# A two-layer RWKV-7 and attention block on one core: the readout products of a chain step ordered behind those of its state

## The chip, the cores and the metric

The kernel runs on 1 core of a Trainium2 chip. The metric is the device time in microseconds (us) of one execution; the median of three runs stands for it. One more execution was taken with the hardware profiler, and every row shown comes from that one.

A core has five engines that run side by side, each with a queue of its own that it works off in order: PE multiplies matrices (PEld are its weight loads), DVE works on vectors, ACT applies functions and copies, POOL is a second, general engine, and SP here only issues DMA transfers. PE writes to PSUM, a small memory that DVE and ACT read; everything else lies in SBUF or, outside the core, in DRAM.

## The reference, cut to what matters

The block has two layers on one residual stream of 1024 latent tokens and 256 context tokens, 1024 channels wide. Layer 0 mixes the tokens with a bidirectional RWKV-7 recurrence, layer 1 with attention; each is followed by an MLP. The change touches the recurrence of layer 0 alone, which the reference writes as a scan over tokens, for 16 heads of 64 channels, forward and backward:

```python
def _wkv_step(state, inp):
    r, w, k, v, kk, bvec = inp
    sa = jnp.einsum('bhvk,bhk->bhv', state, -kk)
    state = state * w[:, :, None, :] + sa[..., None] * bvec[:, :, None, :] + v[..., None] * k[:, :, None, :]
    y = jnp.einsum('bhvk,bhk->bhv', state, r)
    return state, y

def _rwkv_scans(p, init_f, init_b):
    r, v, g, kk, dirs = p
    (dec_f, k_f, a_f), (dec_b, k_b, a_b) = dirs
    s_f, y_f = wkv_scan(r, dec_f, k_f, v, kk, kk * a_f, init_f, False)
    s_b, y_b = wkv_scan(r, dec_b, k_b, v, kk, kk * a_b, init_b, True)
    return s_f, s_b, y_f + y_b
```

## The kernel before

The scan over single tokens is replaced by one over chunks of 32 tokens: 40 chunks (8 of the context, 32 latent), each a *step* of a *chain*. The 16 heads are cut into four groups of four (two channel tiles `ct2` by two halves `h`), and a `Chain` (line 820) carries one group forward and backward at once. So a step works on eight units: two tiles, two halves, two directions `d`. Two chains run side by side, first groups 0 and 1, then groups 2 and 3: 160 steps in all.

A step (`Chain.step`, line 838) has four products of PE, each of eight calls, one for each unit. In fp32 the trace shows two instructions for one call.

- **X** (line 854): the chunk's inputs against the stacked rows `SV`, which hold the state (64 rows), the values V and the corrections U. It goes to `ps_x`, and ACT copies it to SBUF (line 856).
- **U** (line 860): X times an inverse 32 by 32 triangular matrix `T`. It goes to the other half of `ps_x`. Four copies, one for each 32 partitions, put it into `SV` (line 867, ACT, in the first half of a pass one of the four on DVE).
- **S** (line 874): the next state, from all rows of `SV`, into `ps_s`. DVE multiplies it with the decay and writes it into the state rows of the next `SV` (line 878, one instruction for each half). It isn't needed in the last step.
- **Y** (line 883): the readout of the step, from the same `SV`, into `ps_y`. ACT copies it to `y` (line 886), or, once the other direction has been there, DVE adds it (line 888).

X, U and Y are calls with 32 columns of weights, S with 64; all contract over 128 rows. The next step's X needs the new state; nothing in the chain needs Y.

`T` is the inverse spread over a matrix that is zero outside its 32 partitions (`inverses`, line 831, POOL). It is made for step s + 1 once step s has used its own, since each of the two chains has one buffer of it (`bp`, line 785).

The buffers in PSUM: `px` with two for X and U, `pss` with two for S, `py` with one for Y (line 786), beside three that others hold at that time: eight banks in all.

The data of two steps is loaded at once (`Lanes.load`, line 805): `ST` (1152 KB: the inputs of both chains, with the inverses), `LS` (twice 256 KB: weights of S) and `SV` (eight times 32 KB: the rows V), 11 DMA issues on SP. Each has two buffers, so the load for the next pair can go out when the last step that read the same buffer is done with it: `LS` when S is, `SV` and `ST` when Y is.

What sets the order: `staggered` (line 912) starts the second chain half a step behind the first, and `weave` (line 209) mixes in other work: while groups 0 and 1 run, the rest of the preparation (`Prep`: products, vector work and inverses for the later groups); while groups 2 and 3 run, parts of the readout (`Readout`: centring and scaling of y). The order of each engine's queue isn't this program order, though: a scheduler picks it when the kernel is built, from a simulated timeline, by program order among what is ready then. `k.order(late, early)` (line 136) ties one instruction behind another in that choice, without a semaphore.

Of the kernel before, what the change touches and what calls it, by code (L numbers as in the profile page):

```python
# [9 lines left out]
F32 = mybir.dt.float32  # L10
# [101 lines left out]
class K:  # L112


    def __init__(self, tc, I, O, ctx, dbg):
        self.tc, self.nc, self.I, self.O, self.ctx, self.dbg = tc, tc.nc, I, O, ctx, dbg
        self.const = ctx.enter_context(tc.tile_pool(name="const", reuse_waits="tile", bufs=1))
        self.dram = ctx.enter_context(tc.tile_pool(name="dram", reuse_waits="tile", bufs=1, space=DRAM))
        self.c, self.S, self.tables = {}, {}, None
        self.trail = collections.deque(maxlen=LAG)  # L120
# [654 lines left out]
class Lanes:  # L775
# [3 lines left out]
    def __init__(self, k, es):  # L779
        tc, nc = k.tc, k.nc  # L780
        sb = lambda n, b: es.enter_context(tc.tile_pool(name=n, reuse_waits="tile", bufs=b))
        ps = lambda n, b: es.enter_context(tc.tile_pool(name=n, reuse_waits="tile", bufs=b, space=PSUM))
        vp = sb("vp", 1)
        self.gp, self.xp = sb("gp", 2), sb("xp2", 2)
        self.bp = sb("bp", 1)
        self.px, self.pss, self.py = ps("px", 2), ps("pss", 2), ps("py", 1)
        self.SV = [vp.tile([128, 2, 2, 4, 2, 64], F32, name=f"SV{b}", tag=f"SV{b}") for b in range(2)]
        self.LS = [vp.tile([128, 2, 2, 2, 2, 64, 2], F32, name=f"LS{b}", tag=f"LS{b}") for b in range(2)]
        for b, a, h in itertools.product(range(2), range(2), range(2)):
            q = QUAD[a, h] * 32  # L790
            nc.vector.memset(self.SV[b][q:q + 32, h, a], 0.0)
        for t in self.LS:
            for h in range(2):
                rows = slice(h * 64, h * 64 + 64)
                eye = k.c["ident"][rows, rows].unsqueeze(1).unsqueeze(3).to_broadcast([64, 8, 64, 2])
                nc.scalar.copy(t[rows, h].rearrange("p l d a e c -> p (l d a) e c"), eye)
        self.ST = {}
# [22 lines left out]
class Chain:  # L820
# [17 lines left out]
    def step(self, s):  # L838
        k, nc, pr, L = self.k, self.k.nc, self.pr, self.L
        i, c = divmod(s, 2)  # L840
        both = lambda c: slice(c, 4 - c, 3 - 2 * c)
        gf, gb = self.seq[i]
        rev, lp, ln = gf > gb, pr // 2, pr % 2
        ST, ls, SV = L.ST[lp, i], L.LS[i % 2], L.SV[i % 2]
        stack = lambda ct2, h, d, o: ST[:, ln, h * 4 + ct2 * 2 + d, c, o:o + 32]
        sv = lambda h, ct2, d: SV[:, h, ct2, 2 * d + (c ^ d), ln, :]
        units = [(ct2, h, d) for d in range(2) for ct2 in range(2) for h in range(2)]
        if s == 0:
            self.inverses(0)
        T = self.T  # L850
        xu = L.px.tile([128, 2, 2, 64], F32, name="ps_x", tag="xu")
        for ct2, h, d in units:
            q = QUAD[ct2, h] * 32
            nc.tensor.matmul(xu[q:q + 32, 0, d, :], stack(ct2, h, d, 0), sv(h, ct2, d), start=True, stop=True, tile_position=(0, q))  # L854
        X = L.xp.tile([128, 2, 64], F32, name="X", tag=f"X{ln}")
        L.copied = nc.scalar.copy(X, xu[:, 0])
        yield
        for ct2, h, d in units:
            q = QUAD[ct2, h] * 32
            nc.tensor.matmul(xu[q:q + 32, 1, d, :], T[:, d, q // 32, :], X[:, d, :], start=True, stop=True, tile_position=(0, q))  # L860
        lo, hi = sorted((2 * gf + c, 2 * gb + 1 - c))
        first = lo not in self.seen
        self.seen |= {lo, hi}
        for ct2 in range(2):
            for h in range(2):
                q = QUAD[ct2, h] * 32
                (nc.vector.tensor_copy if first and ct2 == h == 0 else nc.scalar.copy)(SV[q:q + 32, h, ct2, both(c), ln, :], xu[q:q + 32, 1])  # L867
        yield
        if s + 1 < self.n:
            self.inverses(s + 1)  # L870
            i2, c2 = divmod(s + 1, 2)
            pst = L.pss.tile([128, 2, 2, 64], F32, name="ps_s", tag="s")
            for ct2, h, d in units:
                nc.tensor.matmul(pst[h * 64:h * 64 + 64, ct2, d, :], ls[:, h, ln, d, ct2, :, c], sv(h, ct2, d), start=True, stop=True, tile_position=(0, h * 64))  # L874
            for h in range(2):
                rows = slice(h * 64, h * 64 + 64)
                pt = k.c["PT"][rows, pr * 2:pr * 2 + 2, :, s + 1].unsqueeze(3).to_broadcast([64, 2, 2, 64])
                nc.vector.tensor_tensor(L.SV[i2 % 2][rows, h, :, both(c2), ln, :], pst[rows], pt, ALU.mult)  # L878
        yield
        psy = L.py.tile([128, 2, 64], F32, name="ps_y", tag="y")  # L880
        for ct2, h, d in units:
            q = QUAD[ct2, h] * 32
            L.last = nc.tensor.matmul(psy[q:q + 32, d ^ rev, :], stack(ct2, h, d, 32), sv(h, ct2, d), start=True, stop=True, tile_position=(0, q))  # L883
        o = self.y[:, lo:hi + 1:hi - lo, :]
        if first:
            nc.scalar.copy(o, psy)
        else:
            nc.vector.tensor_tensor(o, o, psy, ALU.add)
# [606 lines left out]
```

## Time and profile before

| | |
|---|---|
| median of 3 runs | 4176.76 us (4176.29 to 4187.85) |
| profiled execution | 4175.26 us, its span 4173.5 us |
| PE busy | 3815.4 us (91%) |
| DVE busy | 2206.2 us (53%) |
| ACT, POOL busy | 1503.9 us, 1493.4 us (36% each) |
| DMA, mean over the span | 99 GB/s |
| mean granted clock of PE | 0.922 |

The span is the time from the first to the last instruction of the profiled execution; busy times are of that span. The granted clock is the share of its full speed at which PE was allowed to run. A row of the timeline has the start in us, the length in us, the engine, the line of the kernel, the operation, what is written and read, the shapes and the count of instructions that were merged; in brackets stands how long the engine had been idle before and what ended that. A row of the waits has who waited for whom, the us in total, how many times and the longest. The chain steps run from 862 to 1570 us of the span; ahead of them lie projections and preparation, behind them the output projection, the MLP and the second layer.

### The profile page before, as it was taken

The page shows a single profiled execution, that of the slowest core. Times are in us where ns is not written, and L with a number is a line of the kernel's source. Part 1 is how long each engine was busy: PE and PEld are TensorE (multiplying, and loading weights), DVE is VectorE, ACT ScalarE, POOL GpSimd, SP SyncE. Part 2 cuts the span into 40 slices and gives each one's busy share as a digit, 9 for nine tenths or more (in the row PEclk, how much of TensorE's full clock was granted, in tenths as well). Part 3 has the DMA queues.
Part 4 walks back from the last instruction along what each step waited for, and adds up shares of the span by engine and source line. Part 5 has one row for each costly group of instructions (what it writes and reads, how often), then busy time and mean ns, then how long its engine had stood idle before and what let it go on. Part 6 is the DMA issues. An engine that isn't in the chain of part 4 may idle for free.

```text
span 4173.5 us, 70565 instructions
## 1 busy us (share of the span) xinstructions
PE 3815.4 (91%) x28100; PEld 2915.1 (70%) x28100; DVE 2206.2 (53%) x3705; ACT 1503.9 (36%) x3215; POOL 1493.4 (36%) x1395
## 2 busy tenths in 40 slices
PE   6999768767898998999999999989999999999998
PEld 3667647655666666888888888776444477888886
DVE  6347898878745446443333333648666534333324
ACT  4666555444243333322222222333444422221122
POOL 3124785644424233311111111123778722222221
PEclk8999868856598989999999999999999999999999
DMA  7457867776454444401111111433110021111112
GB/s 276 150 182 178 201 154 173 176 186 155 119 173 134 135 126 133 146 27 39 39 40 39 38 38 39 162 84 108 31 31 16 19 78 41 48 44 48 48 51 71
DMA packets 398202, 414.78 MB, mean 99 GB/s; under 512 B 153504, under 2 KB 303264, under 8 KB 392624
## 3 DMA queue, kind: packets, MB, share of 16 engines
q1 hardware_dynamic: 396912, 408.94, 34.2%
q8 instruction: 222, 3.64, 0.4%
q0 software_dynamic: 960, 1.31, 0.2%
q14 instruction: 108, 0.88, 0.1%
HBM read 294.99 MB, written 117.11 MB: 99 GB/s over the span
## 4 chain that ended last, share of the span: by engine, by line
PE 62%; DVE 5%; DMA 2%; ACT 1%; issue 1%; POOL 0%; SPq 0%; DVEq 0%; POOLq 0%; ACTq 0%
PE ps_pj L271 43%; PE ps_av L1361 4%; PE ps_s L874 3%; PE ps_m L1238 2%; PE ps_s L1401 2%; PE ps_pj L290 2%; PE ps_s L1402 2%; PE ps_y L883 2%; DVE SV L878 2%; PE ps_x L854 1%; DMA ro_v<-d_V 0%; PE ps_su L1372 0%; PE ps_q L1275 0%; POOL w_lo L255 0%; DMA SV<-d_V 0%
## 5 line engine op out<-in xcount | busy, mean ns | idle before, releaser
L255 POOL TENSOR_TENSOR w_lo<-w_raw,w_hi 128x512 fp32r<-128x512 f32 (+1 forms) x292 | 478.3, 1639 | 1693.1 <-ACT w_hi L253 1671.8
L271 PE MATMUL ps_pj<-xh,w_hi 128*128 128x512 f32 (+1 forms) x1712 | 626.7, 367 | 6.4 <-ACT w_hi L253 6.0
L271 PE MATMUL ps_pj<-xl,w_hi 128*128 128x512 f32 (+1 forms) x1712 | 622.5, 364 | 1.0 <-DVE xl L1004 1.0
L271 PE MATMUL ps_pj<-xh,w_lo 128*128 128x512 f32 (+1 forms) x1712 | 617.6, 364 | 5.3 <-POOL w_lo L255 5.2
L1119 DVE SCALAR_TENSOR_TENSOR xr<-ps_pj,c_mod,xr 128x512 f32<-128x512 f32 (+1 forms) x368 | 251.9, 686 | 577.1 <-PE ps_pj L271 576.4
L253 ACT CAST w_hi<-w_raw 128x512 fp32r<-128x512 f32 (+1 forms) x292 | 216.7, 742 | 843.8 <-PE ps_pj L271 626.5
L271 PE MATMUL ps_pj<-hid_l,w_hi 128*128 128x512 f32 (+1 forms) x1280 | 474.4, 371 | 0.0
L271 PE MATMUL ps_pj<-hid_h,w_hi 128*128 128x512 f32 (+1 forms) x1280 | 473.2, 371 | 0.0
L271 PE MATMUL ps_pj<-hid_h,w_lo 128*128 128x512 f32 (+1 forms) x1280 | 469.8, 370 | 0.0
L1143 DVE TENSOR_TENSOR m_q<-m_r 128x512 f32<-128x512 f32 x160 | 183.8, 1150 | 418.2 <-ACT m_r L1141 417.9
L271 PEld LDWEIGHTS ps_pj<-xh,w_hi 128*128 128x128 f32 x1712 | 324.5, 190 | 61.1 <-ACT w_hi L253 7.8
L271 PEld LDWEIGHTS ps_pj<-xh,w_lo 128*128 128x128 f32 x1712 | 322.4, 189 | 59.1 <-POOL w_lo L255 8.1
L271 PEld LDWEIGHTS ps_pj<-xl,w_hi 128*128 128x128 f32 x1712 | 324.3, 190 | 53.4 <-DVE xl L1004 1.8
L1412 POOL TENSOR_TENSOR acc<-acc,p 128x1024 f32<-128x1024 f32 x122 | 295.4, 2421 | 58.8 <-ACT p L1405 54.4
L874 PE MATMUL ps_s<-SV,LS 128*64 128x64 f32 x2496 | 248.1, 266 | 30.9 <-DVE SV L867 23.8
L271 PEld LDWEIGHTS ps_pj<-hid_h,w_hi 128*128 128x128 f32 x1280 | 241.3, 189 | 44.2
L271 PEld LDWEIGHTS ps_pj<-hid_h,w_lo 128*128 128x128 f32 x1280 | 241.1, 188 | 43.9
L271 PEld LDWEIGHTS ps_pj<-hid_l,w_hi 128*128 128x128 f32 x1280 | 241.4, 189 | 43.2
L878 DVE TENSOR_TENSOR SV<-ps_s,c_PT 64x256 f32<-64x256 f32 x312 | 131.4, 421 | 228.4 <-PE ps_s L874 222.4
L1405 ACT ACTIVATE p<-ps_s 128x1024 f32<-128x1024 f32 x160 | 163.8, 1024 | 230.5 <-PE ps_s L1402 229.8
L271 PE MATMUL ps_pj<-xlo,w_hi 128*128 128x512 f32 (+1 forms) x576 | 226.0, 393 | 12.6 <-DVE xlo L480 12.5
L874 PEld LDWEIGHTS ps_s<-SV,LS 128*64 128x64 f32 x2496 | 170.5, 161 | 90.2 <-DVE SV L867 30.0
(235 smaller groups left out, 7269.8 us busy)
## 6 DMA issues: line engine op xcount, KB each, us to landing
ST<-d_ST SPq DMA_DIRECT2D x40, 1152.0 KB
wmod<-in_wmod SPq DMA_DIRECT2D x32, 1024.0 KB
w_raw<-in_m SPq DMA_DIRECT2D x64, 512.0 KB
w_raw<-in_m SPq DMA_DIRECT2D x128, 256.0 KB
d_ST<-AR SPq DMA_DIRECT2D x160, 128.0 KB
d_LS<-KT SPq DMA_DIRECT2D x320, 64.0 KB
d_ST<-G SPq DMA_DIRECT2D x160, 128.0 KB
LS<-d_LS SPq DMA_DIRECT2D x80, 256.0 KB
```

Source lines behind the costliest of these rows:

```text
L253: nc.scalar.copy(hi, raw)
L255: getattr(nc, eng).tensor_tensor(lo, raw, hi.bitcast(F32), ALU.subtract)
L271: i = nc.tensor.matmul(ps[:, :n], w[:, sl], x[:, t0:t0 + n], start=a, stop=z)
L290: nc.tensor.matmul(ps[:, :n], w[:, sl], x[:, t0:t0 + n], start=a, stop=z)
L874: nc.tensor.matmul(pst[h * 64:h * 64 + 64, ct2, d, :], ls[:, h, ln, d, ct2, :, c], sv(h, ct2, d), start=True, stop=True, tile_position=(0, ...
L878: nc.vector.tensor_tensor(L.SV[i2 % 2][rows, h, :, both(c2), ln, :], pst[rows], pt, ALU.mult)
L883: L.last = nc.tensor.matmul(psy[q:q + 32, d ^ rev, :], stack(ct2, h, d, 32), sv(h, ct2, d), start=True, stop=True, tile_position=(0, q))
L1119: k.nc.vector.scalar_tensor_tensor(x[:, t0:t0 + n], ps[:, :n], g, x[:, t0:t0 + n], ALU.mult, ALU.add)
L1143: nc.vector.tensor_tensor(q[:, :n], r[:, :n], r[:, :n], ALU.mult)
L1361: line(nc.tensor.matmul(st["av"][e * 64:e * 64 + 64], k.V[:, kt, ct // 2 * 64:ct // 2 * 64 + 64], p[:, e], start=(kt == 0), stop=(kt == 9) ...
L1405: nc.scalar.activation(p, ps, AF.Exp)
L1412: (nc.vector if ct == KT - 1 and kt % 3 == 2 else nc.gpsimd).tensor_tensor(st["acc"], st["acc"], p, ALU.add)
```

## The change

It does three things.

1. Each Y call of a step is ordered behind the last S call of that step (where there is one).
2. Y gets no tile of its own: it is written into a third part of the tile that holds X and U. The pool `py` goes, and `px` has three buffers in place of two.
3. The pool `bp` of `T` has two buffers in place of one.

```diff
         self.gp, self.xp = sb("gp", 2), sb("xp2", 2)
-        self.bp = sb("bp", 1)
-        self.px, self.pss, self.py = ps("px", 2), ps("pss", 2), ps("py", 1)
+        self.bp = sb("bp", 2)
+        self.px, self.pss = ps("px", 3), ps("pss", 2)
...
-        xu = L.px.tile([128, 2, 2, 64], F32, name="ps_x", tag="xu")
+        xu = L.px.tile([128, 3, 2, 64], F32, name="ps_x", tag="xu")
...
             pst = L.pss.tile([128, 2, 2, 64], F32, name="ps_s", tag="s")
             for ct2, h, d in units:
-                nc.tensor.matmul(pst[h * 64:h * 64 + 64, ct2, d, :], ls[:, h, ln, d, ct2, :, c], sv(h, ct2, d), start=True, stop=True, tile_position=(0, h * 64))
+                last = nc.tensor.matmul(pst[h * 64:h * 64 + 64, ct2, d, :], ls[:, h, ln, d, ct2, :, c], sv(h, ct2, d), start=True, stop=True, tile_position=(0, h * 64))
...
         yield
-        psy = L.py.tile([128, 2, 64], F32, name="ps_y", tag="y")
+        psy = xu[:, 2]
         for ct2, h, d in units:
             q = QUAD[ct2, h] * 32
-            L.last = nc.tensor.matmul(psy[q:q + 32, d ^ rev, :], stack(ct2, h, d, 32), sv(h, ct2, d), start=True, stop=True, tile_position=(0, q))
+            i = nc.tensor.matmul(psy[q:q + 32, d ^ rev, :], stack(ct2, h, d, 32), sv(h, ct2, d), start=True, stop=True, tile_position=(0, q))
+            if s + 1 < self.n:
+                k.order(i, last)
```

## The prediction

> **What bounds the kernel now.** I read the page first: PE ends the run and holds most of the chain that ended last.
>
> ```profile
> span 4173.5 us, 70565 instructions
> PE 62%; DVE 5%; DMA 2%; ACT 1%; issue 1%; POOL 0%; SPq 0%; DVEq 0%; POOLq 0%; ACTq 0%
> ```
>
> The diff touches only the chain steps, which run between 862 and 1570 us, so the rest of the page can't move by itself. I cut that stretch into seven stages (A to G, in this order) and counted X's copy, L856, which stands once in each of the 160 chain steps. Columns: stretch, its length, ACT busy (count), granted clock, DMA share, GB/s.
>
> ```profile
> 862.00:1147.00 285.00, 10.19 (x40) 0.60 0.61 150
> 1147.00:1215.00 68.00, 6.65 (x25) 1.00 0.58 177
> 1215.00:1302.00 87.00, 6.59 (x26) 0.96 0.51 156
> 1302.00:1374.00 72.00, 3.84 (x16) 0.74 0.39 117
> 1374.00:1505.00 131.00, 9.83 (x39) 1.00 0.45 139
> 1505.00:1552.00 47.00, 2.57 (x10) 0.64 0.46 137
> 1552.00:1570.00 18.00, 1.27 (x5) 1.00 0.28 83
> ```
>
> Length over count is the price of a step: A 7.1 us, B 2.7, C 3.35, D 4.5, E 3.36, F 4.7, G 3.6. C, E and G repeat one pattern. This is one step of it, from X to the next X, in the timeline of E (each call of fp32 stands as two instructions, so x16 is one set of eight calls):
>
> ```profile
> 1405.85 0.44 PE L860 MATMUL ps_x<-X,T 128*32 128x64 f32 x13
> 1406.23 0.30 PE L854 MATMUL ps_x<-SV,ST 128*32 128x64 f32 x2
> 1406.66 0.30 DVE L867 COPY SV<-ps_x 32x128 f32<-32x128 f32 x1
> 1406.99 0.82 ACT L867 COPY SV<-ps_x 32x128 f32<-32x128 f32 x3 [0.63 <-DVE SV L867]
> 1407.04 0.33 PE L874 MATMUL ps_s<-SV,LS 128*64 128x64 f32 x2
> 1407.31 0.30 PE L883 MATMUL ps_y<-SV,ST 128*32 128x64 f32 x2
> 1407.72 0.25 ACT L856 COPY X<-ps_x 128x128 f32<-128x128 f32 x1
> ...
> 1408.52 0.57 PE L874 MATMUL ps_s<-SV,LS 128*64 128x64 f32 x10
> 1409.02 0.45 SPq L813 DMA_DIRECT2D LS<-d_LS  x1
> 1409.03 0.35 PE L883 MATMUL ps_y<-SV,ST 128*32 128x64 f32 x9
> 1409.13 0.88 DVE L878 TENSOR_TENSOR SV<-ps_s,c_PT 64x256 f32<-64x256 f32 x2 [2.17 <-PE ps_s L874]
> 1409.60 0.30 PE L854 MATMUL ps_x<-SV,ST 128*32 128x64 f32 x2
> ```
>
> See that S (L874, 64 columns) and Y (L883, 32 columns) take turns, one call each: three turns in 1.48 us (1407.04 to 1408.52), 0.49 each; only then do five calls of S stand together. S takes 1407.04 to 1409.03, 1.99 us. It isn't the U copies that pace the turns: they end some 0.27 us apart (0.82 for three) and are all done at 1407.81. And DVE waits 2.17 us for S before it can form the next state. Stage B shows the same instructions without turns, in the chain that comes second:
>
> ```profile
> 1191.44 0.70 PE L874 MATMUL ps_s<-SV,LS 128*64 128x64 f32 x16
> 1192.08 0.49 PE L854 MATMUL ps_x<-SV,ST 128*32 128x64 f32 x16
> 1192.46 0.43 PE L883 MATMUL ps_y<-SV,ST 128*32 128x64 f32 x16
> 1192.79 0.30 PE L854 MATMUL ps_x<-SV,ST 128*32 128x64 f32 x2
> ```
>
> There a whole S takes 0.64 us up to the next form, a whole Y 0.33.
>
> **The change part by part.**
>
> **Y behind S.** No instruction is added. Eight Y calls move behind the last S call of their step, so the three turns go. The wait is one of order on PE alone; behind Y stands U of the other chain, which needs X's copy and that isn't late (1407.72). Y also releases the SV and ST buffers to SP: it now ends some 0.5 us behind S, while SP is at the two issues of LS (1.09 us, below): covered. S and Y cost 0.64 + 0.33 = 0.97 us of PE, against 1.99 plus the five Y calls that already stand behind (5/8 of 0.33, 0.21): 2.20. That is 1.2 us less PE a step at full clock. Not all of it is time, for two loops come next.
>
> The first is the loop through the copies: U's end, four copies in a row (1406.66 to 1407.81, 1.15 us), the five S calls that need the last copy (0.51 with the change of form), Y 0.33, the next U 0.44, and some 0.1 for hand-overs: 2.5 us. In half of the steps the first copy sits on DVE behind L878; with 0.2 more there I take 2.6.
>
> The second is the load of the next pair of steps, which has two buffers: LS goes out when the last S that reads the buffer is done, and then ST and SV.
>
> ```profile
> 1181.77 0.43 PE L854 MATMUL ps_x<-SV,ST 128*32 128x64 f32 x9 [0.33 <-DMA SV<-d_V]
> 1192.17 1.09 SPq L813 DMA_DIRECT2D LS<-d_LS  x2
> 1201.30 1.42 POOL L836 TENSOR_TENSOR T<-ST,c_qmask 128x256 f32<-128x256 f32 x2 [5.78 <-DMA ST<-d_ST]
> 1202.94 0.49 PE L854 MATMUL ps_x<-SV,ST 128*32 128x64 f32 x16
> ```
>
> From LS's issue ST has landed after 9.1 us (1192.17 to 1201.30), SV comes behind it, and X starts after 10.8; at 1181.77 it already waits 0.33 for SV. So the load takes between 9.2 and 10.7 us. In E the next LS starts 2.8 us behind an X (1406.23 to 1409.02) and four steps of 3.37 make 13.5: 10.7 are left, so the load is only just hidden. After the change S ends about 1.1 us behind X (X 0.38, S 0.64, a hand-over), and four steps can't be under 1.1 + 9.2 to 1.1 + 10.7, 10.3 to 11.8: 2.6 to 2.95 a step. I take 2.85, nearest to the row in which X waits. C and E: 65 steps by 0.5, **32.5 us** (between 65 by 0.3 and by 0.85). G has no load behind it: 5 by 0.7, **3.5**. In B one chain of two takes turns and the load is the limit already (10.9 for four): 0.1 by 25, **2.5** (0 to 9).
>
> Stages A, D and F have other work on DVE and a clock that falls to half. What a step pays there:
>
> ```profile
> 1351.69 1.12 PE L874 MATMUL ps_s<-SV,LS 128*64 128x64 f32 x16
> ...
> 1527.81 0.48 PE L874 MATMUL ps_s<-SV,LS 128*64 128x64 f32 x2
> 1530.92 0.53 PE L883 MATMUL ps_y<-SV,ST 128*32 128x64 f32 x9
> ```
>
> S with turns takes 3.1 us (1527.81 to 1530.92), S in one piece 1.12, 1.6 times the 0.70 of B: DVE gets S up to 2 us earlier. Whether it can use that is in its waits for S in A, D and F (us, times, longest):
>
> ```profile
> DVE SV L878 <- PE ps_s L874: 24.3, 11, 5.6
> DVE SV L878 <- PE ps_s L874: 15.5, 11, 2.2
> DVE SV L878 <- PE ps_s L874: 12.4, 5, 3.5
> ```
>
> These are the bounds from above; below it is nothing, if DVE's next instruction waits as long for another. A: 11 waits by 1.7, **19**. D: 11 by 1.2 (part of it at full clock), **13**. F: ten steps at 4.7 could come to 3.3 (the copy loop at half clock: 1.6 times the 1.28 us of S, Y and U, copies 1.15, hand-overs 0.1), 14 us, but DVE's waits allow **12**.
>
> **Y in the tile of X and U, one more buffer.** No bank is added: two and one become three. The tile now lives until y has been taken out, and its buffer is asked for again three steps later, 8 us and more: covered. What goes is the wait of Y for the single buffer. **T double buffered:** POOL's waits for U go; nearly no one waits for T.
>
> ```profile
>   DVE y L888: 4.4, 8
>   PEld ps_x L860: 2.2, 2
> ```
>
> The first is PE's idle time before Y, over the whole run, the second its weight loads' wait for T (us, times). Gains of 0 to 4.4 and 0 to 2.2 us, if what follows doesn't wait for the copies anyway; in C and E, where the copies pace it, that is so. I take 0 for both; POOL's own idle time before T is off the path.
>
> The Trainium skill, "PSUM — Partial Sum Buffer", "Summary: rules for kernel authors", advises another bank, or at least another quadrant, for what PE writes while one is read, and semaphores by bank: that speaks against this tile. By it Y must wait until the copies have read U (1.15 us), which S ahead of it waits for anyway, and no row of before shows such a wait; only the four last steps have no S, so the sum would be 4 us more by it at most.
>
> **The sum:** 19 + 2.5 + 32.5 + 13 + 12 + 3.5 = 82.5 us. The profiled execution took 4175.26 us (span 4173.5 and 1.8 around it); 4175.3 - 82.5 = 4092.8. The median of the runs shown is 1.5 above the profiled one, so 4094.
>
> **The rivals.**
>
> **The load doesn't bind.** If the load takes 9.2 us, or the order brings both chains side by side as in B, the copy loop's 2.6 or less stands: C and E 65 by 0.8, 52; B 9, A, D and F at their bounds, 52; G 4: 117 in all, **4060**. For it: 9.1 us is all that ST needs. Against it: the wait at 1181.77. Chance 0.17.
>
> **The clock falls.** PE will have gaps in each step. F's clock is half for long, although PE is busy:
>
> ```profile
> 1516.00:1549.00 33.00, 31.44 (x428) 22.07 (x428) 14.00 (x35) 9.12 (x37) 11.68 (x13) 0.50 0.47 137
> ```
>
> At half clock the copy loop gives 3.3 us a step, and C, E and G save nothing in place of 36: **4130**. Against it: B packs a step into 2.7 us and keeps 1.00. Chance 0.15. The Trainium skill, "TensorE: Matmul & The Clock Gate", "Why this matters for your kernels", would not expect it: only gaps above some 3 us bring the clock down. The row above speaks against that rule: PE is busy 31.44 of 33 us at 0.50.
>
> **The turns stay with another partner (slower).** The order is made from a simulated timeline when the kernel is built. With Y shut out, it may put U or X of the other chain into the gaps between S calls while the copies run. Then three turns (1.48 us) stay, and Y comes behind S as a piece of its own: 0.33 - 0.21 + a change of form of about 0.15, some 0.25 more a step, 40 us over 160: **4216**. The point at which it decides: X's copy must be out ahead of the third U copy. Now it stands behind all of them on ACT (1407.72). Chance 0.05.
>
> **The change doesn't shorten S.** The same refilling in a part of the steps, or every stage waits for something else by then: **4170**, chance 0.08.
>
> **How the numbers follow.** Forecast 0.55 (4094, from 4070 to 4125); load free 0.17; clock 0.15; no gain 0.08; slower 0.05. The range of 8 in 10 goes from 4045 (117 and some of the small gains) to 4142 (C and E at 0.3, A at nothing). About 0.3%, 12.5 us, is what a measurement of this kernel can tell from no change: faster 0.55 + 0.17 + 0.15 = 0.87, within it 0.08, slower 0.05.
>
> **What would show it.** S as one group x16 of about 0.64 us in E, with Y x16 behind it. E's steps near 2.85 us, and an X each fourth step that waits for DMA SV or ST; DVE's wait for S in E well under 2.17 us. E's clock still 1.00. If E's steps come to 2.6 without such waits, the load was over-priced; if S still stands in pairs, the forecast is wrong; if A doesn't shrink, DVE was its bound.

## The result, and the profile after

The changed kernel takes 4124.73 us (median of 4 runs, 4121.08 to 4128.73), the kernel before took 4178.0 beside it: a ratio of 0.9868, 95% interval 0.985 to 0.9886, so 53 us faster. The forecast was 82.5 us less and 4094, so the sum was some 30 us too large; its range, 4045 to 4142, holds the time. The profiled execution after is the slowest of its four (4128.73), the one before the fastest of its own, so the two profiles lie only 46.6 us apart.

The page after, span and chain of the work that ended last:

```profile
span 4126.9 us, 70535 instructions
PE 58%; DVE 3%; DMA 3%; ACT 1%; issue 1%; POOL 1%; SPq 1%; DVEq 0%; POOLq 0%; ACTq 0%
```

PE's share of the chain falls from 62% to 58%, DMA's rises from 2% to 3%. That alone doesn't tell that the steps wait for transfers: the page after puts 1% on `ro_v`, which belongs to the readout, and 0% on `SV`, as before. For the stages, cut both kernels at the same steps, from X copy to X copy (40 steps, 25, 26, 16, 39, 10; the last three are G). First before, then after, each row with its length, ACT's copies of X (count), granted clock, DMA share and GB/s.

```profile
866.00:1149.60 283.60, 10.19 (x40) 0.60 0.60 148
1149.60:1217.40 67.80, 6.65 (x25) 1.00 0.61 185
1217.40:1304.80 87.40, 6.59 (x26) 0.96 0.51 154
1304.80:1377.20 72.40, 4.08 (x16) 0.74 0.36 111
1377.20:1509.20 132.00, 9.84 (x39) 1.00 0.48 146
1509.20:1556.10 46.90, 2.57 (x10) 0.64 0.39 112
```

```profile
874.00:1146.70 272.70, 10.13 (x40) 0.59 0.63 151
1146.70:1225.20 78.50, 6.36 (x25) 0.86 0.56 164
1225.20:1306.70 81.50, 6.61 (x26) 0.83 0.57 170
1306.70:1370.60 63.90, 4.19 (x16) 0.73 0.42 127
1370.60:1480.10 109.50, 10.39 (x39) 0.95 0.60 182
1480.10:1518.60 38.50, 2.62 (x10) 0.78 0.43 122
```

| stage | steps | before | after | saved | forecast |
|---|---|---|---|---|---|
| A | 40 | 283.6 | 272.7 | 10.9 | 19 |
| B | 25 | 67.8 | 78.5 | -10.7 | 2.5 |
| C | 26 | 87.4 | 81.5 | 5.9 | 13 |
| E | 39 | 132.0 | 109.5 | 22.5 | 19.5 |
| D | 16 | 72.4 | 63.9 | 8.5 | 13 |
| F | 10 | 46.9 | 38.5 | 8.4 | 12 |
| G | last 3 | 10.1 | 5.3 | 4.8 | 3.5 |

The chain as a whole is 50.3 us shorter (C and E had one term, 32.5). It begins 8 us later (874.1 against 866.1) and what lies behind it is 4.2 us shorter: 50.3 - 8.0 + 4.2 = 46.5, which is 46.6 before rounding. Three things strike: B pays what A gains, C gains little, and E gains more than its share. The timeline of E after shows a pair of steps:

```profile
1425.76 1.23 PE L874 MATMUL ps_s<-SV,LS 128*64 128x64 f32 x16
...
1426.91 0.43 PE L883 MATMUL ps_x<-SV,ST 128*32 128x64 f32 x16
...
1427.27 0.70 PE L874 MATMUL ps_s<-SV,LS 128*64 128x64 f32 x16
...
1428.00 1.09 SPq L813 DMA_DIRECT2D LS<-d_LS  x2
...
1429.69 0.27 ACT L856 COPY X<-ps_x 128x128 f32<-128x128 f32 x1 [2.01 <-PE ps_x L854]
```

S stands as x16, its second chain in 0.70 us, and Y behind it: the turns are gone, as forecast. But see the two S, 1.5 us apart (1425.76 and 1427.27): both chains do the same step **side by side**, where E before had them half a step apart. So the last S of a pair of steps is done early, and the next LS goes out at 1428.00, ahead of the first X copy that follows (1429.69). B after is the opposite:

```profile
1161.01 1.09 SPq L813 DMA_DIRECT2D LS<-d_LS  x2
...
1170.49 2.79 POOL L836 TENSOR_TENSOR T<-ST,c_qmask 128x256 f32<-128x256 f32 x4 [9.86 <-DMA ST<-d_ST]
...
1172.09 0.30 PE L854 MATMUL ps_x<-SV,ST 128*32 128x64 f32 x2 [0.25 <-DMA SV<-d_V]
1172.48 0.27 ACT L856 COPY X<-ps_x 128x128 f32<-128x128 f32 x1 [1.04 <-PE ps_x L854]
1173.05 1.09 SPq L813 DMA_DIRECT2D LS<-d_LS  x2
```

Here LS goes out 0.6 us behind the X copy (1172.48 to 1173.05), both ST (POOL's 9.86 us) and SV (PE) are waited for, and from LS to LS four steps take 12.04 us. In B before, the two chains stood side by side. In B and C, PE waits for SV 1.2 us before and 16.1 after (a row of the waits of each, over B and C: us, times, longest):

```profile
PE ps_x L854 <- DMA SV<-d_V: 1.2, 2, 0.9
```

```profile
PE ps_x L854 <- DMA SV<-d_V: 16.1, 17, 2.9
```

**The theory to test:** four steps take at least *load* (from LS's issue to the X copy that needs it) plus *lag* (from that X copy to the next LS). Where that X doesn't wait for a transfer, the load as measured here holds some slack. The lag depends on how the two chains stand to each other, not on how long S is. The main rival is that of the prediction: the turns themselves set the time.

### The profile page after: what moved, and what is told of

It is laid out like the page before. It is cut to its first block, busy times and chain, and to the rows that moved or that the text cites. A ratio compares the mean times of both kernels' runs of the same rounds, so it can differ in the third digit from the quotient of the medians.

```text
span 4126.9 us, 70535 instructions
## 1 busy us (share of the span) xinstructions
PE 3727.7 (90%) x28100; PEld 2866.8 (69%) x28100; DVE 2201.4 (53%) x3705; ACT 1506.7 (37%) x3215; POOL 1489.1 (36%) x1395
## 4 chain that ended last, share of the span: by engine, by line
PE 58%; DVE 3%; DMA 3%; ACT 1%; issue 1%; POOL 1%; SPq 1%; DVEq 0%; POOLq 0%; ACTq 0%
PE ps_pj L271 43%; PE ps_av L1363 4%; PE ps_m L1240 2%; PE ps_s L1403 2%; PE ps_pj L290 2%; PE ps_s L1404 2%; DMA ro_v<-d_V 1%; DMA wmod<-in_wmod 0%; PE ps_s L874 0%; DMA SV<-d_V 0%; PE ps_su L1374 0%; POOL w_lo L255 0%; PE ps_n L356 0%; DMA K<-K 0%; PE ps_mod L192 0%
## 5 line engine op out<-in xcount | busy, mean ns | idle before, releaser
L271 PEld LDWEIGHTS ps_pj<-xh,w_lo 128*128 128x128 f32 x1712 | 322.9, 190 | 61.5 <-POOL w_lo L255 10.4
L271 PE MATMUL ps_pj<-xlo,w_hi 128*128 128x512 f32 (+1 forms) x576 | 225.0, 392 | 13.7 <-DVE xlo L480 13.6
L271 PE MATMUL ps_pj<-xhi,w_hi 128*128 128x512 f32 (+1 forms) x576 | 224.9, 398 | 7.7 <-ACT xhi L479 6.3
L1244 DVE TENSOR_REDUCE mc<-ps_m 128x1 f32<-128x512 f32 x256 | 174.8, 690 | 99.0 <-PE ps_m L1240 95.3
L271 PE MATMUL ps_pj<-xhi,w_lo 128*128 128x512 f32 (+1 forms) x576 | 220.7, 384 | 7.4 <-POOL w_lo L255 7.2
```

Source lines behind the costliest of these rows:

```text
L271: i = nc.tensor.matmul(ps[:, :n], w[:, sl], x[:, t0:t0 + n], start=a, stop=z)
L1244: line(nc.vector.tensor_reduce(mc[:, t + u, t0 // 512:t0 // 512 + 1], ps, AX.X, ALU.max), "v")
```

## The experiments

The medians, and the ratios to the kernel before, which ran beside each:

| kernel | us | ratio | 95% interval | chain in the profile |
|---|---|---|---|---|
| changed kernel | 4124.73 | 0.9868 | 0.985 to 0.9886 | 649.9 |
| e1 order alone | 4159.96 | 0.9958 | 0.9942 to 0.9973 | 673.6 |
| e2 tile and T alone | 4120.0 | 0.9862 | 0.9843 to 0.9882 | 646.6 |
| e3 order and tile | 4116.89 | 0.9853 | 0.9828 to 0.9878 | 639.6 |
| e10 before, one tick | 4143.08 | 0.9909 | 0.9886 to 0.9933 | 668.4 |
| e5 before, no load | 4166.61 | 0.9976 | 0.9962 to 0.9989 | 685.7 |
| e13 order alone, no load | 4087.91 | 0.9797 | 0.9779 to 0.9815 | 601.3 |
| e4 changed, no load | 4086.56 | 0.9776 | 0.9757 to 0.9796 | 604.3 |
| e6 changed, one tick | 4112.37 | 0.9837 | 0.982 to 0.9853 | 641.2 |
| e7 changed, three ST | 4108.18 | 0.984 | 0.9816 to 0.9864 | 615.1 |
| e11 three ST, one tick | 4102.64 | 0.9835 | 0.9821 to 0.9849 | 625.4 |
| e12 the same, one T | 4105.06 | 0.9835 | 0.9819 to 0.9852 | 615.3 |

### Which part of the change does it: e1, e2, e3

e1 is the kernel before with the order alone:

```diff
-                nc.tensor.matmul(pst[...
+                last = nc.tensor.matmul(pst[...
...
-            L.last = nc.tensor.matmul(psy[...
+            y = nc.tensor.matmul(psy[...
+            if s + 1 < self.n:
+                k.order(y, last)
```

> The kernel before with the order alone: each Y call behind the last S call of its step; Y keeps its own PSUM tile, T its single buffer. Theory 'the order ends the turns': S stands in one group of 16 instructions of 0.64 to 0.70 us in stage E and the time is that of the changed kernel, 4115 to 4135 us. Rival 'the shared tile ends them, the order is redundant': S and Y still take turns somewhere and the time stays above 4160 us. Rival 'the order is needed, but the single y buffer now costs': S stands in one group, PE waits ahead of Y for y's copy in most steps, and the time is 4135 to 4160 us.

e2 is the changed kernel without it:

```diff
-            if s + 1 < self.n:
-                k.order(i, last)
```

> The changed kernel without the order of Y behind S; Y lies in the tile of X and U, T has two buffers. Theory 'the order ends the turns': S and Y take turns as before, S takes about 2 us in E, and the time is 4165 to 4185 us. Rival 'the shared tile does it as well' (Y writes the tile that the U copies read, so the planner sees Y as ready only behind them): S in one group of 0.7 us, Y behind it, and a time of 4115 to 4135 us.

e3 is the changed kernel with T's second buffer taken back:

```diff
-        self.bp = sb("bp", 2)
+        self.bp = sb("bp", 1)
```

> The changed kernel with one buffer of T in place of two. Prediction's step 'T double buffered is worth 0': within 6 us of the changed kernel, 4118 to 4131 us. Rival 'the second buffer of T moves the planner's order': a difference of more than 12 us to either side, with stages B or C in another order (two steps side by side, or half a step apart).

e2 and e3 can't be told from the changed kernel: the intervals overlap. (e3's median, 4116.89, lies 1.1 us below its expected band; its four runs go from 4107.56 to 4123.39.) So the order of Y behind S, the change's first part, is not needed, and T's second buffer is worth nothing that these runs can tell. e2's S stands as x16 too: the shared tile ends the turns by itself (or with T's buffer, which was not tried apart; e3 has the tile without it). Y's calls write the tile that the U copies still read, and the planner places Y behind them.

The traces say more than that. PE, ACT, DVE and POOL work in e2 through the same operations in the same order as in the changed kernel (PE in 28090 of 28100 places; the other ten are neighbours that changed places). So these are two profiles of one order, and they show how far a stage scatters from one profile to the next: A 272.7 and 275.3 us, D 63.9 and 66.5, and E 109.5 and 103.6. This is E in e2:

```profile
1369.30:1472.90 103.60, 10.40 (x39) 0.94 0.64 193
```

e1's time lies at the edge of its third expectation, but not by the mechanism named there. The timeline of E in e1 (Y isn't late; the waits for SV are):

```profile
1421.90 0.27 ACT L856 COPY X<-ps_x 128x128 f32<-128x128 f32 x1 [4.80 <-PE ps_x L854]
...
1422.89 1.54 PE L874 MATMUL ps_s<-SV,LS 128*64 128x64 f32 x16
...
1424.26 1.61 SPq L813 DMA_DIRECT2D LS<-d_LS  x2
...
1434.89 0.53 PE L854 MATMUL ps_x<-SV,ST 128*32 128x64 f32 x9 [0.26 <-DMA SV<-d_V]
...
1435.61 0.27 ACT L856 COPY X<-ps_x 128x128 f32<-128x128 f32 x1 [4.10 <-PE ps_x L854]
```

The turns are gone (x16), and E still takes 130.6 us, against 132.0. PE now waits for SV. This order pairs the last step of one chain's pair with the first of the other chain's next pair, so the S that frees LS comes behind the X that has waited: LS goes out 2.4 us behind the X copy (1421.90 to 1424.26), the load takes 11.35 (to 1435.61), together 13.7 for four steps. The load took the place of the turns at the same height.

### Turns or place: e10

The kernel before, with turns, tiles and buffers as they were, but both chains started in the same tick of the program order:

```diff
-            if t >= 4 * l and (t - 4 * l) % 8 in STAGES:
+            if t % 8 in STAGES:
```

> The kernel before, Y's tile, buffers and order as they were, with both chains started in the same tick. In E the order then has both chains side by side, and S and Y take turns in one of the two chains only (in C in both still). Theory 'in E the place of the two chains to each other was worth the gain, not the turns by themselves': E falls from 132 to 103 to 112 us, C stays near 87, and the time is 4140 to 4160 us. Rival 'the turns were': E keeps half of them and loses half of its gain at most, 118 to 126 us, and the time is 4160 to 4172 us. Rival 'neither, the shared tile itself': no change, 4172 to 4180 us.

E of e10, in the timeline:

```profile
1431.86 0.33 PE L874 MATMUL ps_s<-SV,LS 128*64 128x64 f32 x2
...
1432.12 0.30 PE L883 MATMUL ps_y<-SV,ST 128*32 128x64 f32 x2
...
1433.34 0.57 PE L874 MATMUL ps_s<-SV,LS 128*64 128x64 f32 x10
...
1434.18 0.70 PE L874 MATMUL ps_s<-SV,LS 128*64 128x64 f32 x16
...
1434.91 1.09 SPq L813 DMA_DIRECT2D LS<-d_LS  x2
...
1435.64 0.27 ACT L856 COPY X<-ps_x 128x128 f32<-128x128 f32 x1 [1.08 <-PE ps_y L883]
```

The three turns are there, 1.48 us from 1431.86 to 1433.34, in one chain of the two, and E is 107.8 us (its row stands with the next ones), no longer than after the change. LS is out ahead of the X copy (1434.91 and 1435.64). C, which keeps turns in both chains here, stays at 84.7 against 87.4. So in E the whole gain comes with the chains side by side, although one chain of the two keeps its turns. Place and turns aren't fully apart here, since the other chain lost its turns by the same edit. And the turns that are left may cost some us: 107.8 here, against 109.5 and 103.6 in the two profiles of the changed order.

### The two floors, one by one: e5, e13, e4

These three leave out the loads from the third pair of steps of each group on:

```diff
     def load(self, k, g, i):
...
+        if i > 1:
+            self.ST[g, i] = self.ST[g, i - 2]
+            return
```

> The kernel before without the same loads (the steps use what the first two loads left). Theory 'before the change the turns paced C and E, with the load just hidden': C and E stay at 3.3 to 3.4 us a step (E 128 to 132 us), and the time is 4155 to 4177 us. Rival 'the load paced them already, and the turns only filled its wait': E falls to 2.6 to 3.0 us a step, 100 to 117 us, and the time is below 4150 us.

> The kernel before with the order of Y behind S alone (Y's own tile, T's single buffer) and without the loads of ST, LS and SV from the third pair of steps of each group on; the steps use what the first two loads left. Fourth corner of turns by loads in E: 131.9 us with both, 130.5 without the turns, 133.5 without the loads. Theory 'two floors of one height': with neither, E falls to 95 to 112 us, C from 77 to 65 to 72, and the time is 4085 to 4115 us. Rival 'the order with the chains one step apart is what holds E up (Y's single buffer, PE's waits for copies)': E stays above 122 us.

> The changed kernel without the loads of ST, LS and SV from the third pair of steps of each group on; the steps use what the first two loads left (transfers are left out, every engine instruction stays). Theory 'the load paces B and C': with the order of the changed kernel, B falls from 78 to 60 to 66 us and C from 81 to 62 to 68, E from 109 to 92 to 100, the time is 4070 to 4095 us. Rival 'the copies and the products pace them': B and C lose less than 5 us each, 4110 to 4131 us.

The rows of stage E (the stages as above), of e1, e10, e5, e13 and e4, one kernel a fence:

```profile
1366.20:1496.80 130.60, 10.38 (x39) 0.81 0.50 149
```

```profile
1377.60:1485.40 107.80, 10.36 (x39) 0.99 0.61 184
```

```profile
1370.80:1504.20 133.40, 9.80 (x39) 0.98 0.01 3
```

```profile
1332.80:1425.00 92.20, 10.39 (x39) 0.98 0.02 4
```

```profile
1337.20:1431.00 93.80, 10.38 (x39) 0.97 0.02 4
```

Read E as a square of four, turns by loads:

| E, us | with the loads | without |
|---|---|---|
| both chains with turns | 132.0 (before) | 133.4 (e5) |
| no turns | 130.6 (e1) | 92.2 (e13) |

Taking away either alone saves nothing; taking both saves 40 us. (e5 and e13 lie just outside the bands expected of E, 128 to 132 and 95 to 112, each on the side of its theory; e4's C, 71.6, lies above its 62 to 68.) The turns and the load are two floors of about one height, 13.5 us for four steps. Each row compares one order with itself, with and without the loads. Down a column the order changes too, from half a step apart to one step apart, so 13.6 is the load's floor in e1's order; in the order of before it was not measured. e4 gives the same for the changed kernel: without the loads B falls from 78.5 to 62.9 us, C from 81.5 to 71.6, E from 109.5 to 93.8, so the load paces all three after the change. B and C of e4:

```profile
1141.80:1204.70 62.90, 6.25 (x25) 0.98 0.06 16
1204.70:1276.30 71.60, 6.57 (x26) 0.95 0.21 58
```

### Lifting the load: e7, e6, e11, e12

e7 gives ST a third buffer and loads it one pair of steps earlier (the new function issues what `load` issued for ST before):

```diff
-        self.gp, self.xp = sb("gp", 2), sb("xp2", 2)
+        self.gp, self.xp = sb("gp", 3), sb("xp2", 2)
...
+        self.load_st(k, g, 0)
+        self.load_st(k, g, 1)
+
+    def load_st(self, k, g, i):
+        if i < len(Chain.seq):
+            ST = self.ST[g, i] = self.gp.tile([128, 2, 9, 2, 64], F32, name="ST", tag="ST")
+            k.nc.sync.dma_start(...
...
+                self.L.load_st(self.k, self.pr // 2, s // 2 + 2)
```

> The changed kernel with three buffers of ST in place of two, and ST's load issued one pair of steps earlier; LS and SV keep two. Theory 'the load of the next two steps paces B and C of the changed kernel (12 to 13.8 us for four steps)': with 1152 of the 1920 KB of a load out of that loop, LS's issue to SV's landing falls from some 11 us to about 4, PE's waits for SV fall from 23 us to below 8, B and C come from 3.1 to 2.4 to 2.7 us a step (10 to 25 us less in the two), and the time is 4090 to 4115 us. Rival 'the staggered order paces them, the load only hides it': PE waits for something else by then and the time stays at 4118 to 4131 us. Rival 'the queues are full': the load takes as long as before, since all of it shares 16 queues, and the time is the same.

e6 is the changed kernel with the one-line edit of e10; e11 has the edits of e6 and e7; e12 has `bp` back at 1 as well.

> The changed kernel with both chains started in the same tick of the program order, in place of half a step apart; the order then has both chains' X, both U, S, Y, S, Y side by side in A, B, most of C and E, where the changed kernel has that in E alone. Theory 'how the two chains stand to each other sets when the load of the next pair goes out': in B and C the issue of LS moves from 0.2 to 0.9 us behind the first X copy of a pair of steps to about 1 us ahead of it, four steps take 10.2 to 11 us in place of 12 to 13.8, B and C are 8 to 20 us less together, E stays at 103 to 110 us, and the time is 4090 to 4115 us. Rival 'side by side has its own bound there' (B and C have other work on DVE and POOL): B and C stay, 4118 to 4131 us. Rival 'side by side is bad where DVE is the bound': A grows by more than 10 us, the time is above 4131 us.

> The changed kernel with three buffers of ST and both chains started in the same tick. Here the order pairs the same step of both chains in A and B, but in D, E and F the last step of one chain's pair with the first of the other's next (one step apart). Theory 'what pairing decides is when LS and SV go out': with ST loaded earlier only 768 KB are left in that loop, so E still takes 100 to 110 us, and the time is 4085 to 4110 us. Rival 'one step apart costs by itself, whatever the load': E goes back above 120 us and the time is above 4112 us.

> The same (three buffers of ST, both chains in the same tick) with one buffer of T: the order then has the same step of both chains side by side from A to F. Theory 'load and order together': A as with both chains in one tick (266 us or less), B and C 70 us each, E 99 to 104, F 38: the time is 4080 to 4105 us, the fastest of all. Rival 'three buffers of ST are all of it, one tick adds nothing': 4101 to 4116 us.

B and C of e7, then of e6:

```profile
1144.40:1214.80 70.40, 6.61 (x25) 0.89 0.66 191
1214.80:1285.90 71.10, 6.74 (x26) 0.95 0.63 177
```

```profile
1139.00:1219.40 80.40, 6.61 (x25) 0.82 0.58 168
1219.40:1297.60 78.20, 6.83 (x26) 0.85 0.59 170
```

e7 saves 8.1 us in B and 10.4 in C against the changed kernel, and no X waits for SV there on PE. Its planned order changed too (side by side in B), so the two causes are not apart in e7. They are in the medians over E (nine times four steps; load and lag from the trace as defined above, each a median of its own):

| E | load | lag | X copy to X copy |
|---|---|---|---|
| before | 12.20 | 1.30 | 13.50 |
| e1 | 11.31 | 2.26 | 13.57 |
| after | 11.49 | -1.19 | 10.34 |
| e10 | 11.38 | -0.62 | 10.65 |
| e11 | 8.35 | 1.96 | 10.31 |

e11 is the test: in E its chains stand one step apart like those of e1 (lag 1.96), but with ST out of the loop its load is 8.35 us, and E takes 100.7. It has the shared tile beside that; e13, which hasn't, says the same: without loads, one step apart, E is 92.2 there, and 93.8 side by side (e4). One step apart costs nothing by itself; it costs what the load makes of it. The load fell less than the "about 4" that was expected ahead of e7: SP's rows for the issues of LS and SV alone take 1.09 and 4.81 us.

e6 failed in part: its B, side by side, got no shorter (80.4 us). The rows fit other work of A that reaches further into B: A is 6.9 us shorter, and the last L717 of the preparation starts at 1150.28 us, with 44 copies of X done, where the changed kernel has 1141.16 and 40. e11 and e12 are alike, and their B stays at 79.9 and 81.1 us, where 70 had been expected of e12. This was argued from the rows and not tried.

Of the kernels with all their loads e11 has the lowest median, but e7, e11 and e12 can't be told apart, so nothing shows that the one-tick start adds to three ST buffers. All three ratios (0.9835 to 0.984) are lower than that of the changed kernel (0.9868), and the intervals of e11 and of the changed kernel just don't meet; but that of e2, which runs the same order, meets all three. So what the third buffer is worth in time is left open; in the profiles the chain is 21 to 35 us shorter with it.

## Why the prediction was right, and where it was not

**Y behind S shortens S: right.** S stands as x16 in nearly every step from B on (in A many steps still have it in pieces), the second chain's in 0.70 us in E, and the DVE waits for it shrink.

**"That is 1.2 us less PE a step ... two loops come next": right in form.** e5 and e13 bear out that the turns paced E before with the load just hidden, and that the load is next.

**C and E, "after the change S ends about 1.1 us behind X": the step that failed in E.** LS is free when the *later* chain is done with it. With the chains one step apart, that S comes behind the first X of the next pair, however short it is: in e1, where the turns are gone, LS goes out 2.26 us behind X's copy. In the changed kernel the planner moved the chains of E side by side, and LS goes out 1.19 us ahead of it. The prediction had that move only as a clause of the rival "the load doesn't bind". The load itself was sized about right for E (9.2 to 10.7 us forecast up to X; in e1 10.6 to the end of the last wait for SV, 1424.26 to 1434.89, and 11.35 to X's copy).

In C it is the other way round. There the chains stay half a step apart, and LS goes out 0.7 us behind X's copy (median of its six loads), which is about the 1.1 behind X that was forecast. But the load was sized too short: it takes 11.0 to 12.4 us up to X's copy in three loads of C, and four steps take 11.7 to 13.0, where the forecast had 11.4. SP puts out the `SV` transfers late there: over B and C its queue waits 31.0 us ahead of them, with the landing of `ST` as the last event, and in E of the same profile it has no such wait. Why it waits was not tried.

So C got 5.9 us in place of 13, and E 22.5 in place of 19.5: the sum, 28.4 of 32.5, came out nearly right by luck.

**B, "the load is the limit already ... 2.5 (0 to 9)": wrong in sign.** Before, B took 67.8 us with the loads and 68.9 without them (e5), so the load was not its limit. After, the planner set the chains half a step apart in B, the lag went from -0.62 to 0.99 us (medians of six loads), and the load became its limit: 62.9 us without it (e4).

**A, 19: the wait went, the time did not.** DVE's two largest waits up to the end of the preparation, before and then after (us, times, longest):

```profile
DVE SV L878 <- PE ps_s L874: 20.3, 9, 5.6
DVE sgw L630 <- ACT sgw L623: 16.6, 9, 2.6
```

```profile
DVE sgw L630 <- ACT sgw L623: 23.7, 12, 4.1
DVE SV L878 <- PE ps_s L874: 9.0, 5, 2.7
```

And the last instructions of the preparation on DVE (L717) in the two timelines, before and after:

```profile
1134.72 3.69 DVE L717 STREAM_TRANSPOSE TTo<-Tn 128x1024 f32<-128x1024 f32 x2
```

```profile
1141.16 3.64 DVE L717 STREAM_TRANSPOSE TTo<-Tn 128x1024 f32<-128x1024 f32 x2 [2.72 <-POOL To L712]
```

DVE waits 11.3 us less for S and 7.1 us more for ACT's sgw, and the preparation ends 267.1 us behind the first X copy (1141.16 - 874.1) in place of 268.6 (1134.72 - 866.1). The chain only got two steps further by then (40 copies of X in place of 38). A and B together are 351.4 us before and 351.2 after: of 21.5 us forecast for the two nothing came. The lower bound that the prediction kept ("if DVE's next instruction waits as long for another") is what happened, with B giving back the rest.

**D and F, 13 and 12: right in mechanism, mis-sized,** 8.5 and 8.4. The order alone (e1) brings 5.7 and 6.6, and e2, with the order of the changed kernel, 5.9 and 9.2, so what the tile adds there can't be told. G gave 4.8 for 3.5.

**"Y in the tile of X and U ... 0": the largest surprise of the parts.** The tile is what carries the result (e2, with T's buffer). The Trainium skill, "PSUM — Partial Sum Buffer", "Summary: rules for kernel authors", speaks for another bank than the one being read; the prediction counted what comes of sharing as a cost of 4 us at most. In e2's trace Y stands behind the copies, and there that is the gain: Y could not slip between the S calls. T's buffer made no difference that could be told, as forecast (e3).

**The rivals.** The clock did fall, to 0.86 and 0.83 in B and C and 0.95 in E, but with the gaps of the load: without the loads it is 0.98, 0.95 and 0.97 in the same stages (e4), so it follows the load here. From B on the turns did not come back with U or X as partner. The slower end was not near.

## What to carry to other kernels

Two floors of one height hide each other: taking away the one that shows (the turns) is worth nothing until the other (a double-buffered load) is seen, so work out every loop's length and ask how far apart they are. Where several streams share one load, its next issue waits for the *last* reader: what counts is how the streams stand to each other. And when a scheduler makes the order, a small edit (a tile shared) can move whole stages into another order, for better in one and for worse in the next; compare the orders before crediting the edit.

## What the runs showed that was not expected

**Turns between calls of one width cost nothing.** In E after, Y and the next X, both of 32 columns, alternate by one or a few calls:

```profile
1423.04 0.32 PE L883 MATMUL ps_x<-SV,ST 128*32 128x64 f32 x8
1423.17 0.22 PE L854 MATMUL ps_x<-SV,ST 128*32 128x64 f32 x1
...
1423.19 0.26 PE L854 MATMUL ps_x<-SV,ST 128*32 128x64 f32 x3
...
1423.51 0.23 PE L883 MATMUL ps_x<-SV,ST 128*32 128x64 f32 x2
```

All 32 instructions of the two sets end by 1423.74, 0.70 us, no more than a Y of 0.33 and an X of 0.38 in one piece, while a turn between 64 and 32 columns takes 0.49 us for two calls (e10 above). Y and X write different tiles too, so the rows point to the change of width as what costs; no run takes it apart.

**PE stands for up to 3.3 us with no releaser in the trace.** E before takes 13.1 to 13.5 us for four steps, nine times. After, it is 9.6 to 11.1, but twice 12.9 and 13.0, with rows like this one:

```profile
1457.78 0.35 PE L854 MATMUL ps_x<-SV,ST 128*32 128x64 f32 x9 [2.69 <-issue]
```

Such gaps ahead of X come to 7.8 us in E after, 6.1 in e3, 5.4 in e7, 1.2 in e2, and there are none in E before or in e10. Since e2 runs the same order as the changed kernel, the gaps can account for the difference between 109.5 and 103.6 us in E.

The traces hold a hint at what they are. The page lists a DMA queue named `q8 instruction`, whose packets are 16 KB. Over B to F of all thirteen traces PE has 31 such gaps of more than 0.9 us, and 29 of them end 1.25 to 1.68 us after a packet of this queue has landed, though such packets come only each 5.6 to 7.0 us on average. The three kernels without the loads have as many packets (58) and not one such gap, but neither have e1 and e2. This fits PE waiting for its own instructions, which come late while the loads move; it was not tried apart.

**The start of the chain scatters.** In the thirteen traces of before, after and the experiments the first X copy stands anywhere from 866.1 to 878.6 us, though ahead of it the kernel before and the changed one have the same order. Differences of some us between single profiles are no finding; the stages were compared from X copy to X copy for that reason.
